# The 32-row forward substitutions of a hybrid decoder layer, issued on GpSimd (POOL) in place of VectorE (DVE)

## The chip, the cores and the metric

The kernel runs on one core of one Trainium2 chip. The metric is the device time of one execution in microseconds (us). Three executions of the kernel before took 1258.54 to 1261.52 us, median 1260.12 us. One execution was also profiled: it took 1260.07 us, of which 1258.4 us is the span from its first to its last recorded instruction. All times "at ... us" count from the start of that span.

Engines carry these names in the rows: PE is TensorE (matmuls), DVE is VectorE, ACT is ScalarE, POOL is GpSimd, SP is SyncE, which here only issues transfers (SPq is its queue).

## The reference: what is computed

One decoder layer on 256 tokens of width 2048, all in float32: a normalisation, one input product with `w_in`, four mixers side by side (gated delta rule, mLSTM, RG-LRU, RWKV-7), an output product with `w_out`, a SwiGLU feed-forward part, a last normalisation. Two mixers need a triangular solve per chunk. For the gated delta rule the reference says

```
lower = jnp.tril(jnp.einsum('nbhcd,nbhsd->nbhcs', kb, k) * decay, -1)
sol = lax.linalg.triangular_solve(lower + eye, rhs, left_side=True, lower=True, unit_diagonal=True)
```

and RWKV-7 is a scan over time, which the kernel turns into chunks with the same kind of solve.

## The kernel before

**Weights.** Every weight matrix is cut into 396 units of 128 x 1024 numbers. SP loads a unit into a `raw` buffer (4 of them), ACT copies it to `whi` (rounded to the matmul type), DVE computes `wlo = raw - whi`, and PE runs three matmuls for each product: whi with the activations' high part, whi with their low part, wlo with the high part (lines 169 to 171). There are 4 `whi` and 4 `wlo` buffers, so PE can be at most four units behind DVE. A unit of the input product is 24 matmuls, about 3 us of PE. These conversions carry line number 274, whatever engine they are on; a few carry 277. Tile names carry a number: `wlo_2268` is the low half of the unit whose high half is `whi_2267` and whose raw buffer is `raw_2265`.

**Mixers.** Their small work is written as Python generators (`rwkv_half`, `gdn_half`, `mlstm_half`, `rglru_half`, `gates_mm`, `joint_solve`) that are advanced a piece at a time between the units. From that program order, a scheduler with its own idea of how long each instruction takes makes one fixed order for each engine. Each engine then runs its list strictly in that order, and waits where an operand is not there.

**The solve.** `joint_solve` inverts many 32 x 32 unit triangular blocks at once, one block per partition: 64 blocks for RWKV, and later 32 for the delta rule. `blk` holds the blocks (loaded by lines 625 and 933), `inv` starts as the identity, and for each of 31 columns `solve_blocks` does two elementwise operations on 31 to 256 elements per partition: an outer product into `tmp` (line 499) and an addition into `inv` (line 500). Each reads what the one before wrote. Then line 503 writes the transpose of `inv` into `blk` with one copy on DVE, lines 512 and 513 store both to DRAM, and lines 660, 661 (RWKV) and 945, 946 (delta rule) load them back in another layout, for which lines 654, 940 and 941 have cleared the target on POOL.

**Neighbours in the DVE order.** `rglru_half` has the DVE lines 1140, 1150, 1151, 1154, 1155, 1158, 1161 and needs ACT for a square root (line 1152) between 1151 and 1154. `gates_mm` has the DVE lines 811, 814, 817, 818, and a scan at line 819, whose result PE transposes (line 413, tile `mx` from `sD`); ACT does a logarithm for it (line 816). The lines 763 and 774 are the convolution of the next column group and its activation, 1080 to 1088 belong to the mLSTM.

Of the kernel before, what the change touches and what calls it, by code (L numbers as in the profile page):

```python
# [10 lines left out]
ALU = mybir.AluOpType  # L11
# [478 lines left out]
def solve_blocks(em, q0, nq, steps, n=32):  # L490

    nc = em.nc
    blk, inv, tmp = em.blk[q0 : q0 + nq], em.inv[q0 : q0 + nq], em.tmp[q0 : q0 + nq]
    for j in range(n - 1):
        a, b = n - 1 - j, j + 1
        tv = tmp[:, 0 : a * b].rearrange("p (x y) -> p x y", x=a)
        col = blk[:, j, j + 1 : n].unsqueeze(2).to_broadcast([nq, a, b])
        row = inv[:, j, 0:b].unsqueeze(1).to_broadcast([nq, a, b])
        nc.vector.tensor_tensor(tv, col, row, op=ALU.mult)
        nc.vector.tensor_tensor(inv[:, j + 1 : n, 0:b], inv[:, j + 1 : n, 0:b], tv, op=ALU.add)  # L500
        if j % steps == steps - 1:
            yield
    nc.vector.tensor_copy(blk.rearrange("q s t -> q t s"), inv)


def joint_solve(em, key, q0, nq, steps, free=False):
    nc = em.nc
    while not all((key + "A", h) in em.mix for h in range(2)):
        yield
    yield from solve_blocks(em, q0, nq, steps)  # L510
    dt, dtt = (em.dp.tile([nq, 32, 32], F32, name=em.nm("dr"), tag=em.nm("dr")) for _ in range(2))
    nc.sync.dma_start(dt, em.inv[q0 : q0 + nq])
    nc.sync.dma_start(dtt, em.blk[q0 : q0 + nq])
    em.mix[key + "S"] = (dt, dtt)
    if free:
        em.free(*em.solver)
# [960 lines left out]
```

## Time and profile before

| | |
|---|---|
| median of 3 executions | 1260.12 us (1258.54 to 1261.52) |
| the profiled execution | 1260.07 us, span 1258.4 us |
| PE busy | 1237.0 us, 98% of the span |
| DVE busy | 788.2 us, 63% |
| ACT busy | 639.5 us, 51% |
| POOL busy | 32.7 us, 3% |
| substitutions on DVE | 124 instructions, 41.1 us, at 154 to 206 us (RWKV) and 356 to 411 us (delta rule) |
| granted TensorE clock, mean | 0.995 |

PE is busy almost all the time, so what counts is where PE has to wait. A busy share of another engine matters only where PE waits for that engine.

### The profile page before, as it was taken

The page shows a single profiled execution, that of the slowest core. Times are in us where ns is not written, and L with a number is a line of the kernel's source. Part 1 is how long each engine was busy: PE and PEld are TensorE (multiplying, and loading weights), DVE is VectorE, ACT ScalarE, POOL GpSimd, SP SyncE. Part 2 cuts the span into 40 slices and gives each one's busy share as a digit, 9 for nine tenths or more (in the row PEclk, how much of TensorE's full clock was granted, in tenths as well). Part 3 has the DMA queues.
Part 4 walks back from the last instruction along what each step waited for, and adds up shares of the span by engine and source line. Part 5 has one row for each costly group of instructions (what it writes and reads, how often), then busy time and mean ns, then how long its engine had stood idle before and what let it go on. Part 6 is the DMA issues. An engine that isn't in the chain of part 4 may idle for free.

```text
span 1258.4 us, 18347 instructions
## 1 busy us (share of the span) xinstructions
PE 1237.0 (98%) x7216; PEld 1066.3 (85%) x7216; DVE 788.2 (63%) x1096; ACT 639.5 (51%) x849; POOL 32.7 (3%) x65
## 2 busy tenths in 40 slices
PE   9999999999998999999999999999999999999997
PEld 8999999988998688888888888888888888878885
DVE  7896898668689767754454444444445465556554
ACT  7666774447644354644444444444444454455443
POOL 1000000000001010000000000000000000001000
PEclk9999999999999999999999999999999999999999
DMA  8664437363654635566666666666666666666663
GB/s 334 197 198 141 143 112 204 110 201 95 204 163 138 182 113 179 170 197 185 186 198 185 184 193 192 203 207 193 188 190 190 188 191 192 192 190 191 195 192 109
DMA packets 72198, 226.97 MB, mean 180 GB/s; under 512 B 15752, under 2 KB 16016, under 8 KB 72112
## 3 DMA queue, kind: packets, MB, share of 16 engines
q1 hardware_dynamic: 71504, 224.14, 58.3%
q0 software_dynamic: 464, 1.57, 0.5%
q8 instruction: 56, 0.92, 0.3%
q14 instruction: 30, 0.25, 0.1%
q10 hardware_dynamic: 144, 0.10, 0.0%
HBM read 222.49 MB, written 3.28 MB: 179 GB/s over the span
## 4 chain that ended last, share of the span: by engine, by line
PE 93%; DVE 4%; ACT 1%; issue 1%; DMA 0%; DVEq 0%; POOLq 0%; POOL 0%; SPq 0%; ACTq 0%
PE big L171 16%; PE big L170 16%; PE big L169 16%; PE mx L169 10%; PE mx L170 10%; PE mx L171 10%; PE mx L409 5%; PE big L277 2%; PE mxl L171 2%; PE mxl L170 2%; PE mxl L169 2%; DVE wlo L274 1%; PE mx L413 1%; DVE sA L763 0%; DMA sD<-in_xT 0%
## 5 line engine op out<-in xcount | busy, mean ns | idle before, releaser
L274 DVE TENSOR_TENSOR wlo<-raw,whi 128x1024 fp32r<-128x1024 f32 x396 | 485.4, 1227 | 356.5 <-ACT whi L274 355.5
L274 ACT ACTIVATE whi<-raw 128x1024 fp32r<-128x1024 f32 x396 | 417.8, 1057 | 431.0 <-PE big L171 296.5
L170 PE MATMUL big<-wlo,nhi 128*128 128x512 f32 (+1 forms) x464 | 161.4, 348 | 1.2 <-DVE wlo L274 1.2
L169 PE MATMUL big<-whi,nhi 128*128 128x512 f32 (+1 forms) x464 | 161.5, 348 | 0.0
L171 PE MATMUL big<-whi,nlo 128*128 128x512 f32 (+1 forms) x464 | 161.0, 347 | 0.0
L171 PE MATMUL big<-nhi,wlo 128*128 128x256 f32 x512 | 147.9, 289 | 0.0
L170 PE MATMUL big<-nlo,whi 128*128 128x256 f32 x512 | 147.9, 289 | 0.0
L169 PE MATMUL big<-nhi,whi 128*128 128x256 f32 x512 | 147.0, 287 | 0.0
L169 PE MATMUL mx<-whi,nhi 128*128 128x512 f32 x352 | 138.0, 392 | 0.0
L171 PE MATMUL mx<-whi,nlo 128*128 128x512 f32 x352 | 137.0, 389 | 0.0
L170 PE MATMUL mx<-wlo,nhi 128*128 128x512 f32 x352 | 137.0, 389 | 0.0
L170 PEld LDWEIGHTS big<-nlo,whi 128*128 128x128 f32 x512 | 97.7, 191 | 1.9 <-issue 0.7
L171 PEld LDWEIGHTS big<-nhi,wlo 128*128 128x128 f32 x512 | 97.7, 191 | 1.8 <-issue 0.3
L170 PEld LDWEIGHTS big<-wlo,nhi 128*128 128x128 f32 x464 | 88.5, 191 | 12.4 <-DVE wlo L274 1.6
L169 PEld LDWEIGHTS big<-nhi,whi 128*128 128x128 f32 x512 | 97.7, 191 | 1.2 <-issue 0.3
L169 PEld LDWEIGHTS big<-whi,nhi 128*128 128x128 f32 x464 | 88.4, 190 | 10.9
L171 PEld LDWEIGHTS big<-whi,nlo 128*128 128x128 f32 x464 | 88.5, 191 | 10.8
L170 PE MATMUL big<-wlo,sA 128*128 128x512 f32 x220 | 86.5, 393 | 3.7 <-DVE wlo L274 3.7
L169 PE MATMUL big<-whi,sA 128*128 128x512 f32 x220 | 86.7, 394 | 2.0 <-DVE sA L763 1.4
L169 PE MATMUL mx<-whi,sA 128*128 128x512 f32 x208 | 81.5, 392 | 0.7 <-ACT sA L1184 0.7
L170 PE MATMUL mx<-wlo,sA 128*128 128x512 f32 x208 | 81.0, 390 | 0.0
L171 PE MATMUL mx<-whi,sA 128*128 128x512 f32 x208 | 81.0, 389 | 0.0
(436 smaller groups left out, 1805.1 us busy)
## 6 DMA issues: line engine op xcount, KB each, us to landing
raw<-in_units SPq DMA_DIRECT2D x404, 512.0 KB, 3.7
sD<-in_x SPq DMA_DIRECT2D x8, 512.0 KB, 5.1
sD<-in_xT SPq DMA_DIRECT2D x4, 512.0 KB, 6.1
out_y<-sD SPq DMA_DIRECT2D x8, 256.0 KB, 3.0
sA<-in_final_norm POOLq DMA_DIRECT2D x4, 256.0 KB, 4.9
sD<-in_lora SPq DMA_DIRECT2D x1, 512.0 KB, 6.9
sD<-in_rglru POOLq DMA_DIRECT2D x1, 512.0 KB, 4.9
dr<-sD SPq DMA_DIRECT2D x2, 256.0 KB, 4.3
```

The source lines that it names most:

```text
L169: i = nc.tensor.matmul(out, ahi, bhi, start=start, stop=False, skip_group_check=True)
L170: nc.tensor.matmul(out, ahi, blo, start=False, stop=False, skip_group_check=True)
L171: self.last_mm = nc.tensor.matmul(out, alo, bhi, start=False, stop=stop, skip_group_check=True)
L274: i = fn(*a, **k)
L277: i = fn(*a, **k)
L409: return self.em.nc.tensor.matmul(*a, **k)
L413: return self.em.nc.tensor.transpose(*a, **k)
```

## The change

The two operations of each column of `solve_blocks` are issued on GpSimd. The copy of line 503 stays on VectorE.

```
@@ solve_blocks
         col = blk[:, j, j + 1 : n].unsqueeze(2).to_broadcast([nq, a, b])
         row = inv[:, j, 0:b].unsqueeze(1).to_broadcast([nq, a, b])
-        nc.vector.tensor_tensor(tv, col, row, op=ALU.mult)
-        nc.vector.tensor_tensor(inv[:, j + 1 : n, 0:b], inv[:, j + 1 : n, 0:b], tv, op=ALU.add)
+        nc.gpsimd.tensor_tensor(tv, col, row, op=ALU.mult)
+        nc.gpsimd.tensor_tensor(inv[:, j + 1 : n, 0:b], inv[:, j + 1 : n, 0:b], tv, op=ALU.add)
         if j % steps == steps - 1:
             yield
     nc.vector.tensor_copy(blk.rearrange("q s t -> q t s"), inv)
```

The scheduler makes new orders for all engines from this. On DVE, in the stretch of the RWKV solve, the order before had the substitutions strewn between other work (`sD_113` is `inv`, `sD_112` is `blk`, `sD_114` is `tmp`; `sA` and `sB` tiles are the RG-LRU's):

```order
L1140 TENSOR_TENSOR sA_271_2022<-sA_271_2022,sA_244_1801 128x512
L499 TENSOR_TENSOR sD_114_953<-sD_112_951,sD_113_952 64x220
L500 TENSOR_TENSOR sD_113_952<-sD_113_952,sD_114_953 64x22x10
L499 TENSOR_TENSOR sD_114_953<-sD_112_951,sD_113_952 64x231
L500 TENSOR_TENSOR sD_113_952<-sD_113_952,sD_114_953 64x21x11
L499 TENSOR_TENSOR sD_114_953<-sD_112_951,sD_113_952 64x240
L500 TENSOR_TENSOR sD_113_952<-sD_113_952,sD_114_953 64x20x12
L499 TENSOR_TENSOR sD_114_953<-sD_112_951,sD_113_952 64x247
L1150 SCALAR_TENSOR_TENSOR sB_275_2035<-sA_270_2021,sB_275_2035 128x512
```

In the order of the change the same place on DVE holds the copy of the finished inverse (`sD_278` is the gates' tile):

```order
L1140 TENSOR_TENSOR sA_271_2022<-sA_271_2022,sA_244_1801 128x512
L503 COPY sD_112_951<-sD_113_952 64x32x32
L1150 SCALAR_TENSOR_TENSOR sB_275_2035<-sA_270_2021,sB_275_2035 128x512
L814 TENSOR_SCALAR sD_278_2096<-sD_278_2096,gp 16x256
L1151 TENSOR_SCALAR sA_270_2021<-sB_275_2035 128x512
L811 TENSOR_SCALAR sD_278_2096<-sD_278_2096 16x256
L1156 MEMSET sA_274_2034 128x1
L1154 SCALAR_TENSOR_TENSOR sA_270_2021<-sB_275_2035,sA_270_2021 128x512
L1155 TENSOR_TENSOR sA_271_2022<-sA_271_2022,sA_270_2021 128x512
L1158 SCALAR_TENSOR_TENSOR sB_275_2035<-sA_274_2034,sA_271_2022 128x512
L817 TENSOR_TENSOR sD_278_2096<-sD_278_2096 16x256
L1161 TENSOR_TENSOR sB_275_2035<-sB_275_2035,sA_264_1972 128x512
```

The next three rows there are line 818, `wlo_2268` and the scan of line 819. Before, the copy stood 85 rows further down, behind eleven more units' `wlo`; it has moved up to the middle of where the substitutions were.

On DVE in the stretch of the delta rule's solve, before:

```order
L274 TENSOR_TENSOR wlo_4573<-raw_4570,whi_4572 128x1024
L500 TENSOR_TENSOR sD_113_952<-sD_113_952,sD_114_953 32x23x9
L499 TENSOR_TENSOR sD_114_953<-sD_112_951,sD_113_952 32x220
L500 TENSOR_TENSOR sD_113_952<-sD_113_952,sD_114_953 32x22x10
L499 TENSOR_TENSOR sD_114_953<-sD_112_951,sD_113_952 32x231
L500 TENSOR_TENSOR sD_113_952<-sD_113_952,sD_114_953 32x21x11
L274 TENSOR_TENSOR wlo_4620<-raw_4617,whi_4619 128x1024
```

and with the change:

```order
L274 TENSOR_TENSOR wlo_4573<-raw_4570,whi_4572 128x1024
L274 TENSOR_TENSOR wlo_4620<-raw_4617,whi_4619 128x1024
L503 COPY sD_112_951<-sD_113_952 32x32x32
L274 TENSOR_TENSOR wlo_4658<-raw_4655,whi_4657 128x1024
L1080 TENSOR_TENSOR dn_4523<-dn_4523,enm 128x2
```

Here too the copy has moved up, between two units' `wlo`, where before eleven of the 31 columns had been done.

On SP the stores and reloads of the RWKV inverse stood behind `raw_2902` before. With the change they stand between two weight loads ten units earlier (`sD_322` and `sD_326` are the reload targets of the two halves of the heads):

```order
L274 DMA raw_2404<-in_units 128x1024
L512 DMA dr_2510<-sD_113_952 64x1024
L513 DMA dr_2511<-sD_112_951 64x1024
L660 DMA sD_322_2514<-dr_2510 32x8x32 x2
L661 DMA sD_322_2514<-dr_2511 32x8x32 x4
L660 DMA sD_326_2552<-dr_2510 32x8x32
L661 DMA sD_326_2552<-dr_2511 32x8x32 x2
L660 DMA sD_326_2552<-dr_2510 32x8x32
L661 DMA sD_326_2552<-dr_2511 32x8x32
L822 DMA ncd<-sD_278_2096 4x256
L274 DMA raw_2443<-in_units 128x1024
```

On POOL the 62 substitutions of a solve stand in one run, each behind the one before; in the RWKV solve the two clears of line 654 stand among them. PE's order is the same up to the unit of `whi_2736`, ten units behind `whi_2267`; from there on the small matmuls that use the inverse stand earlier.

## Rows read from the trace of the kernel before

**Rows 1.** The page: busy us, share of the span and instructions by engine.

```profile
PE 1237.0 (98%) x7216; PEld 1066.3 (85%) x7216; DVE 788.2 (63%) x1096; ACT 639.5 (51%) x849; POOL 32.7 (3%) x65
```

**Rows 2.** Groups by line, DVE: count | busy us, mean ns of one.

```profile
L499 DVE TENSOR_TENSOR sD<-sD,sD 64x31 f32<-64x31 f32 (+31 forms) x62 | 20.5, 330 | 1.5
L503 DVE COPY sD<-sD 64x1024 f32<-64x1024 f32 (+1 forms) x2 | 2.3, 1126 | 0.0
```

**Rows 3.** Timeline of PE, 395 to 425 us: start, us, [idle before <-releaser].

```profile
403.41 0.52 PE L170 MATMUL big<-wlo,sA 128*128 128x512 f32 x1 [3.73 <-DVE wlo L274]
417.86 0.47 PE L169 MATMUL big<-whi,sA 128*128 128x512 f32 x1 [1.44 <-DVE sA L763]
```

**Rows 4.** Windows: length, busy us by engine, granted clock, DMA share, GB/s.

```profile
400.00:405.00 5.00, 1.59 (x4) 1.27 (x5) 4.73 (x10) 2.79 (x6) 1.34 (x2) 0.88 0.09 21
405.00:410.00 5.00, 5.00 (x21) 3.95 (x20) 4.68 (x11) 3.39 (x7) 0.00 (x0) 0.78 0.71 245
```

**Rows 5.** Timeline of SP, the loads of `blk`; the landing time of line 933.

```profile
146.14 0.31 SPq L625 DMA_DIRECT2D sD<-dr  x1
350.84 0.31 SPq L933 DMA_DIRECT2D sD<-dr  x1
DMA to landing us min/median/max: 3.4/3.4/3.4
```

**Rows 6.** POOL's own operations: timeline, and line 1348's durations.

```profile
3.65 0.45 POOL L307 TENSOR_TENSOR sA<-sA,ident 128x128 f32<-128x128 f32 x1
4.17 0.23 POOL L315 COPY gm<-strict 64x64 f32<-64x64 f32 x1
164.93 0.95 POOL L654 MEMSET sD<- 64x1024 f32 x1 [7.88 <-PE mx L409]
L1348 POOL TENSOR_TENSOR sD<-sD,sA x4: 1444/1740/2242, 1128.1 to 1134.8; 128x512 f32<-128x512 f32 x4
```

**Rows 7.** Timeline of POOL and DVE together, 1127 to 1138 us.

```profile
1130.87 5.65 POOL L1348 TENSOR_TENSOR sD<-sD,sA 128x512 f32<-128x512 f32 x3 [1.29 <-ACT sA L274]
...
1127.21 1.22 DVE L274 TENSOR_TENSOR wlo<-raw,whi 128x1024 fp32r<-128x1024 f32 x1
1130.14 0.69 DVE L1185 TENSOR_TENSOR sA<-sD,sA 128x512 fp32r<-128x512 f32 x1
1131.87 3.49 DVE L1185 TENSOR_TENSOR sA<-sD,sA 128x512 fp32r<-128x512 f32 x2
```

**Rows 8.** Windows ahead of the copy's new places; below, line 499 alone.

```profile
149.50:168.50 19.00, 19.00 (x156) 17.70 (x155) 18.33 (x40) 16.20 (x24) 1.90 (x2) 1.00 0.52 163
354.20:373.50 19.30, 19.30 (x162) 19.25 (x161) 17.58 (x39) 9.35 (x13) 0.00 (x0) 1.00 0.52 158
...
149.50:168.50 19.00, 2.50 (x9) 1.00 0.52 163
354.20:373.50 19.30, 3.32 (x11) 1.00 0.52 158
```

**Rows 9.** Timeline of DVE behind line 1140, and PE's wait point there.

```profile
171.96 0.69 DVE L1150 SCALAR_TENSOR_TENSOR sB<-sA,sB 128x512 f32<-128x512 f32 x1
179.42 0.67 DVE L819 TENSOR_TENSOR_SCAN sD<-sA,sD 16x256 f32<-16x256 f32 x1
...
180.72 0.48 PE L413 MATMUL mx<-ident,sD 16*128 16x16 f32 x5
```

**Rows 10.** Timeline of DVE and PE at `wlo_4658`.

```profile
376.53 1.22 DVE L274 TENSOR_TENSOR wlo<-raw,whi 128x1024 fp32r<-128x1024 f32 x1
...
381.60 0.28 PE L171 MATMUL big<-nhi,wlo 128*128 128x256 f32 x1
```

**Rows 11.** Timeline of SP, store and reload of the RWKV inverse.

```profile
207.75 0.45 SPq L513 DMA_DIRECT2D dr<-sD  x1
212.20 2.77 SPq L661 DMA_DIRECT2D sD<-dr  x6
216.55 0.40 SPq L274 DMA_DIRECT2D raw<-in_units  x1
```

More of the change, by code (lines that the diff above doesn't have):

```diff
@@ L498, in solve_blocks @@
         row = inv[:, j, 0:b].unsqueeze(1).to_broadcast([nq, a, b])
-        nc.vector.tensor_tensor(tv, col, row, op=ALU.mult)
-        nc.vector.tensor_tensor(inv[:, j + 1 : n, 0:b], inv[:, j + 1 : n, 0:b], tv, op=ALU.add)
+        nc.gpsimd.tensor_tensor(tv, col, row, op=ALU.mult)
+        nc.gpsimd.tensor_tensor(inv[:, j + 1 : n, 0:b], inv[:, j + 1 : n, 0:b], tv, op=ALU.add)
         if j % steps == steps - 1:
```

## The prediction, made before the changed kernel had run

> **What bounds the kernel now.** I read the busy times first: PE is busy for 1237 of 1258.4 us [rows 1], so a gain or a loss can only come from PE's waits. The waits of PE show where DVE is late today: PE stood 3.73 us for a `wlo` at 403.4 us and 1.44 us for a convolution at 417.9 us [rows 3]. Both lie in or just behind the stretch of the delta rule's solve, where DVE carries the substitutions beside the weights. After the first one the granted clock is 0.88 and 0.78 in two windows of 5 us, so for a while PE ran at 1.2 instead of 2.4 GHz: (0.12 + 0.22) x 5 = 1.7 us of PE's work lost [rows 4]. In the stretch of the RWKV solve PE waits for nobody: 19.00 of 19.00 us busy [rows 8]. So what DVE can give back is 3.7 + 1.4 + 1.7 = 6.8 us, though the substitutions take 62 x 0.33 us twice on it [rows 2].
>
> **What the change adds: a slow chain on POOL, with DVE waiting in order behind it.** The 62 operations of a solve depend on each other, so POOL does them one by one. Together they have 2 x the sum of (j+1)(31-j) over j = 0 to 30, that is 10,912 elements per partition. POOL's price is read from the two sizes of its own elementwise operations in this trace: 0.448 us (0.45 in the row) for 128 elements, 1.444 us for the fastest with 512 [rows 6]. That makes 1.0 us for 384 elements, 2.59 ns each, and 0.116 us that does not depend on the size. The instruction behind the first of them starts 0.07 us after its end [rows 6]. A solve is then 62 x 0.186 + 10,912 x 0.00259 = 11.5 + 28.3 = 39.8 us; the RWKV one has the two clears among its rows, 0.95 us each [rows 6]: 41.7 us. On DVE one solve took 62 x 0.33 = 20.5 us [rows 2], so POOL needs about twice DVE's time, and nothing of it runs side by side.
>
> When it can start: `blk` is sent for at 146.14 and at 350.84 us, and the second load lands after 3.4 us; with that for both, POOL starts at 149.5 and 354.2 us [rows 5].
>
> To this comes that the two engines hinder each other. While three POOL operations ran back to back, two DVE operations of a kind that alone takes 0.69 us took 3.49 us together, and the three took 5.65 us instead of 3 x 1.44 = 4.33 [rows 6, 7]. So POOL lost 1.3 us beside 2.6 us of DVE's own work (1.2 + 2 x 0.69): half of it. Ahead of the copy's new place DVE has, without the substitutions (18 and 22 of them; line 499 is half), 18.33 - 5.0 = 13.3 us and 17.58 - 6.6 = 10.9 us of work [rows 8]. I charge POOL with half, 6.6 and 5.4 us. DVE itself gets slower there too, but its `wlo` are some units ahead of PE's use (`wlo_4658` began 5.1 us before, [rows 10]), and it is on its way to a wait anyhow.
>
> POOL then ends at 149.5 + 41.7 + 6.6 = 197.8 us, and at 354.2 + 39.8 + 5.4 = 399.4 us.
>
> **Where that hits PE.** In the new DVE order the copy of line 503 stands directly behind line 1140, which DVE reaches about 169 us. DVE stops there for some 28 us. Behind it are, in this order, lines 1150, 814, 1151, the square root on ACT (which has the logarithm and `whi_2267` behind it, so ACT stands too), 1154, 1155, 1158, 817, 1161, 818, `wlo_2268`, and the scan of line 819. Each at its own step in that timeline (0.6 for 1150, 1154, 1155 and 1161, 0.3 to 0.4 for 814, 1151, 817 and 818, 0.7 for ACT with its handover, 1.14 for 1158, 1.13 for the `wlo`, 0.67 for the scan; first and last in [rows 9]) that is 7.4 us. PE's order is unchanged here: at 180.72 us it transposes the scan's result [rows 9], one instruction ahead of the end of its buffered units. So PE stands from 180.7 us until 197.8 + 1.1 (the copy, [rows 2]) + 7.4 = 206.3 us: **25.6 us**.
>
> The second time the copy stands between `wlo_4620` and `wlo_4658`. PE first used `wlo_4658` at 381.6 us, counted in units of 24 matmuls; DVE had made it at 376.5 us [rows 10]. Now it is ready at 399.4 + 1.1 + 1.1 = 401.6 us: **20.0 us**. The next `wlo` has lines 1080 to 1088 before it, some 3.7 us against a unit of 2.7 us on PE: 1.0 us more, an estimate.
>
> Both stalls are longer than the one at 403 us, after which PE lost 1.7 us to the low clock [rows 4]; I take that once for each, 3.4 us.
>
> SP also waits in order behind POOL now. Counted from the RWKV solve's end, the second store goes out at 1.2 us, the reload can start 4.45 us after it, and nine transfers take 4.35 us until a weight load goes out [rows 11]: 10.0 us. That load belongs to the fifth unit after PE's restart; with 3.7 us to land and 2.2 us for both halves it is ready at 16 us, and PE wants it about 22 us after the solve's end. That is hidden with some 6 us of cover; if every landing were 6 us later, SP would become the next wait. The reordered small matmuls of PE come later than that and have their data by then.
>
> **Sum.** 25.6 + 20.0 + 1.0 + 3.4 - 6.8 = +43.2 us. The profiled execution took 1260.07 us, 0.05 us from the median of the three, so the forecast is **1303 us**.
>
> **Bounds.** Without any hindrance it is 12 us less, 1291 us. If DVE's whole work in the two stretches delays POOL, it is 12 us more, 1315 us. POOL's rate: the 1.44 us operation began under a `wlo` that ran until 1128.4 us, 0.3 us after its start [rows 6, 7]; with 1.14 us in its place the rate is 1.8 ns and the fixed part 0.22 us, a solve 37.5 us, 2.3 us less each time. The slowest of the four took 2.24 us, 4.4 ns an element, which with the gaps makes 52 us a solve; it contains the hindrance, so 1291 + 2 x 12.3 = 1316 us. No POOL row reads with a broadcast or in rows of 1 to 31 elements 128 bytes apart, as these do. I take no surcharge, since the second addend's pattern is plain; for the range, half as much again on the 28.3 us is 14.1 us twice, 1332 us. Nothing suggests a gain from the pattern.
>
> **A rule that speaks to this.** The Trainium skill, "SBUF — State Buffer", section "Who interferes with whom", says that a DVE instruction with two SBUF inputs and a GpSimd instruction that reads SBUF shut each other out for their whole length. The doubled DVE operations at 1131.87 us agree with it. By that rule taken fully, the sum would be the 1315 us above instead of 1303.
>
> The Trainium skill, "GPSIMD Engine Reference", section "Elementwise — side-by-side cycle accounting", measures 4497 ns for 2048 elements of such an operation. By that, 2.2 ns an element, the sum would be some 9 us smaller, an estimate.
>
> **Rivals.**
> - *Faster: the chain fits.* If POOL finished the RWKV solve by 180.7 - 7.4 - 1.1 = 172.2 us, and the other by 381.6 - 2.2 = 379.4 us, no copy would hold PE, and DVE's relief would stay: 1260.1 - 6.8 = 1253 us. This needs a solve of at most 22.7 us with the clears, 0.34 us an operation. Against it: DVE itself needs 0.33, and POOL 0.45 for 128 elements where the mean here is 176. Chance 4%.
> - *Full exclusion or a dear pattern.* POOL and DVE take turns over the whole of both stretches, or narrow rows cost half as much again: 1313 to 1335 us. For it: the doubled DVE operations. Against it: POOL's own loss was half. 24%.
> - *A cheap POOL.* The low rate, no hindrance, and waits elsewhere that the stalls swallow (PE has 21 us idle in all): 1265 to 1288 us. 12%.
> - *No change.* The stalls would have to cancel the 6.8 us to within 2.5. 2%.
>
> My forecast, 1288 to 1313 us, has 58%. The range of 1285 to 1332 us holds that, most of the dear cases and a little of the cheap one, some 82%. What a measurement of this kernel can tell from no change is 0.2%, 2.5 us. From the cases above: faster than that 4%, the same 2%, slower 94%.
>
> **What would show it.** In the profile after, POOL should show 124 operations of 0.6 us on the mean and about 75 to 95 us of substitutions. DVE should be idle for 20 to 30 us ahead of each copy of line 503, released by POOL. PE should wait once in the input product for a transpose (line 413) and once for a `wlo`, some 20 to 26 us each, each with a lower granted clock behind it, and the waits at 403 and 418 us should be gone. If POOL's operations take under 0.35 us, or PE's two waits are under 5 us, the prediction is wrong; if the operations take 0.9 us, only its size.

## The result, and the profile of the changed kernel

The changed kernel took **1299.43 us** (median of 4, 1297.42 to 1300.6) against 1260.07 us (median of 4) for the kernel before on the same chip: 39.4 us more, a ratio of 1.031 (95% interval 1.0295 to 1.0325). Its profiled execution took 1297.42 us, with a span of 1295.7 us and a mean granted clock of 0.981.

Busy times on the page of the changed kernel (busy us, share of the span, instructions):

```profile
PE 1240.1 (96%) x7216; PEld 1069.5 (83%) x7216; DVE 755.5 (58%) x972; ACT 639.2 (49%) x849; POOL 109.6 (8%) x189
```

Beside [rows 1], DVE is 33 us lighter, POOL 77 us heavier, and PE has the same number of instructions; the span has grown by 37.3 us and PE's busy time by only 3.1, so PE stood for the rest. The waits of PE say where (total us, times, longest):

```profile
PE mx L413 <- DVE sD L819: 23.4, 1, 23.4
PE big L171 <- DVE wlo L274: 17.8, 1, 17.8
...
PE big L170 <- DVE wlo L274: 1.2, 1, 1.2
```

Two waits hold it all, and the waits of [rows 3] are gone. The third line, 1.2 us, is not the change's work: it stands at 338.56 us, and the kernel before has the same wait of 1.24 us at 311.59 us. Each of the two is read back over DVE to POOL. The timeline of DVE around both, and under it that of PE:

```profile
168.62 0.69 DVE L1140 TENSOR_TENSOR sA<-sA,sA 128x512 f32<-128x512 f32 x1 [1.04 <-ACT sA L1139]
195.66 1.03 DVE L503 COPY sD<-sD 64x1024 f32<-64x1024 f32 x1 [26.36 <-POOL sD L500]
196.54 0.66 DVE L1150 SCALAR_TENSOR_TENSOR sB<-sA,sB 128x512 f32<-128x512 f32 x1
...
203.41 0.67 DVE L819 TENSOR_TENSOR_SCAN sD<-sA,sD 16x256 f32<-16x256 f32 x1
...
422.26 1.43 DVE L503 COPY sD<-sD 32x1024 f32<-32x1024 f32 x1 [25.70 <-POOL sD L500]
423.73 1.22 DVE L274 TENSOR_TENSOR wlo<-raw,whi 128x1024 fp32r<-128x1024 f32 x1
```

```profile
204.14 0.60 PE L413 MATMUL mx<-ident,sD 16*128 16x16 f32 x4 [23.43 <-DVE sD L819]
...
425.00 0.58 PE L171 MATMUL big<-nhi,wlo 128*128 128x256 f32 x1 [17.79 <-DVE wlo L274]
```

DVE has nothing to do with the substitutions any more and yet stands 26.4 and 25.7 us at the copy, with line 1150 and everything behind it in the queue. From the copy's start to the end of the scan, the chain of [rows 9], 8.4 us pass, and PE follows at once. POOL itself, by groups (count | busy us, mean ns | idle before), and in its timeline at the ends and the middle of the two solves:

```profile
L500 POOL TENSOR_TENSOR sD<-sD,sD 64x31 f32<-64x31 f32 (+31 forms) x62 | 39.7, 641 | 4.9
L499 POOL TENSOR_TENSOR sD<-sD,sD 64x31 f32<-64x31 f32 (+31 forms) x62 | 38.2, 616 | 91.8 <-DMA sD<-dr 87.1
```

```profile
148.59 0.23 POOL L499 TENSOR_TENSOR sD<-sD,sD 64x31 f32<-64x31 f32 x1 [11.94 <-DMA sD<-dr]
...
165.53 1.49 POOL L500 TENSOR_TENSOR sD<-sD,sD 64x220 f32<-64x220 f32 x1
...
172.04 0.95 POOL L654 MEMSET sD<- 64x1024 f32 x1
...
185.18 0.61 POOL L500 TENSOR_TENSOR sD<-sD,sD 64x220 f32<-64x220 f32 x1
...
195.39 0.24 POOL L500 TENSOR_TENSOR sD<-sD,sD 64x31 f32<-64x31 f32 x1
...
379.79 0.23 POOL L499 TENSOR_TENSOR sD<-sD,sD 32x31 f32<-32x31 f32 x1 [75.18 <-DMA sD<-dr]
...
400.68 0.61 POOL L499 TENSOR_TENSOR sD<-sD,sD 32x252 f32<-32x252 f32 x1
...
404.26 0.73 POOL L500 TENSOR_TENSOR sD<-sD,sD 32x256 f32<-32x256 f32 x1
...
407.96 0.60 POOL L499 TENSOR_TENSOR sD<-sD,sD 32x247 f32<-32x247 f32 x1
...
421.99 0.24 POOL L500 TENSOR_TENSOR sD<-sD,sD 32x31 f32<-32x31 f32 x1
```

The same operation on 220 elements takes 1.49 us while DVE works and 0.61 us while DVE stands. The sizes of the 31 columns run up and down symmetrically, so one trace gives both prices: in the delta rule's solve the last 13 columns, with DVE idle, took 422.23 - 407.96 = 14.3 us, the middle five 7.3 us, the first 13, of the same sizes but beside DVE for most of the time, 20.9 us. POOL's own time is 2 x 14.3 + 7.3 = 35.8 us, and DVE cost it 6.6 us; in the RWKV solve the first 13 columns took 172.04 - 148.59 = 23.45 us, so 9.2 us.

Windows of 5 us behind the two waits (length, busy us by engine, granted clock, DMA share, GB/s):

```profile
204.00:209.00 5.00, 4.86 (x27) 4.83 (x28) 4.55 (x9) 2.19 (x4) 0.00 (x0) 0.59 0.76 240
425.00:430.00 5.00, 5.00 (x23) 5.00 (x24) 3.14 (x8) 4.11 (x10) 1.37 (x2) 0.50 0.58 193
```

PE comes back at the lower of its two levels, 1.2 GHz, for most of 5 us: 0.41 x 5 + 0.50 x 5 = 4.5 us of work lost.

### The profile page after: what moved, and what is told of

Same layout as the page of the kernel before. It is cut to its first block, busy times and chain, and to the rows that moved or that the text cites. A ratio compares the mean times of both kernels' runs of the same rounds, so it can differ in the third digit from the quotient of the medians.

```text
span 1295.7 us, 18350 instructions
## 1 busy us (share of the span) xinstructions
PE 1240.1 (96%) x7216; PEld 1069.5 (83%) x7216; DVE 755.5 (58%) x972; ACT 639.2 (49%) x849; POOL 109.6 (8%) x189
## 4 chain that ended last, share of the span: by engine, by line
PE 87%; POOL 6%; DVE 2%; issue 2%; ACT 1%; DMA 1%; SPq 0%; DVEq 0%; POOLq 0%; ACTq 0%
PE big L171 15%; PE big L170 15%; PE big L169 15%; PE mx L169 10%; PE mx L171 10%; PE mx L170 10%; PE mx L409 4%; POOL sD L500 3%; POOL sD L499 3%; PE big L277 2%; PE mxl L171 1%; PE mxl L170 1%; PE mxl L169 1%; DVE wlo L274 1%; DMA sD<-dr 0%
## 5 line engine op out<-in xcount | busy, mean ns | idle before, releaser
L171 PE MATMUL big<-nhi,wlo 128*128 128x256 f32 x512 | 150.0, 293 | 17.8 <-DVE wlo L274 17.8
L170 PE MATMUL big<-nlo,whi 128*128 128x256 f32 x512 | 149.5, 292 | 0.0
L171 PEld LDWEIGHTS big<-whi,nlo 128*128 128x128 f32 x464 | 87.7, 189 | 10.9
```

The source lines that it names most:

```text
L170: nc.tensor.matmul(out, ahi, blo, start=False, stop=False, skip_group_check=True)
L171: self.last_mm = nc.tensor.matmul(out, alo, bhi, start=False, stop=stop, skip_group_check=True)
```

## The experiments

Theories. **Order**: the time is waiting, because engines that run a fixed list stand at an instruction that needs POOL's result. **Contention**: the time is POOL and DVE hindering each other, wherever the copy stands. The two are not exclusive: what delays POOL's end also lengthens a wait for it. A third, **queue**, is that SP's stores become the next wait. The ratios are against the kernel before, run on the same chip.

**1. A chain on POOL that nobody waits for.** In the kernel before, behind each two substitutions on DVE (`spare` is a tile of its own, `ones` a constant tile that the rows call `rm`; code cut to the added operations):

```
+        w = min(a * b, 192)
+        nc.gpsimd.tensor_tensor(spare[:, 0:w], blk[:, 0, 0:w] if w <= 32 else ones[:, 0:w], spare[:, 0:w], op=ALU.mult)
+        nc.gpsimd.tensor_tensor(spare[:, 0:w], ones[:, 0:w], spare[:, 0:w], op=ALU.add)
```

> The kernel before, with its substitutions on DVE, and beside them on POOL a chain of 62 dependent operations per solve (up to 192 elements, on a tile of their own, added work that nobody waits for; the output is that of the kernel before). Order theory (the time of the change was lost because DVE's fixed order stands at the copy until POOL has finished): nothing here waits for POOL, so 1260 to 1266 us; the few us are the hindrance making DVE's weights later at 403 us, where PE already waited. Contention theory (the time was lost because POOL and DVE hinder each other at SBUF): POOL reads and writes beside DVE as in the change, DVE even has the substitutions as well, so most of the 39 us comes back: 1285 to 1300 us.

1291.18 us, ratio 1.0258 (1.0236 to 1.0279). Read by the expectation this is the contention theory, and my own reckoning was off by 25 us. The timelines of DVE and POOL at one place, and the group of line 503 (499 before), show more:

```profile
186.76 1.21 DVE L274 TENSOR_TENSOR wlo<-raw,whi 128x1024 fp32r<-128x1024 f32 x1
187.90 0.67 DVE L826 TENSOR_TENSOR_SCAN sD<-sA,sD 16x256 f32<-16x256 f32 x1
```

```profile
186.04 5.84 POOL L507 TENSOR_TENSOR spare<-rm,spare 64x192 f32<-64x192 f32 x1
191.96 0.65 POOL L506 TENSOR_TENSOR spare<-rm,spare 64x192 f32<-64x192 f32 x1
```

```profile
L503 DVE TENSOR_TENSOR sD<-sD,sD 64x31 f32<-64x31 f32 (+15 forms) x31 | 16.0, 516 | 0.4
```

One operation of POOL on 192 elements took 5.84 us while DVE ran its list without a gap, and the next one of the same size 0.65; DVE's substitutions took 516 ns on the mean where [rows 2] have 330. DVE still had its own 62 of them, so it was late for `wlo` and for the gates (PE's longest wait is 7.7 us, for the scan of line 819). (The group covers 148 to 222 us.) Nor is it quite a chain that nobody waits for. Its last multiplication reads `blk`, which DVE's copy overwrites next, and on POOL it stands ahead of `mrs`, a small operation of the mLSTM (line 1089 before) that ACT needs:

```profile
219.99 1.12 DVE L510 COPY sD<-sD 64x1024 f32<-64x1024 f32 x1 [1.81 <-POOL spare L506]
...
413.69 0.69 ACT L1099 ACTIVATE sA<-sA,mrs 128x128 f32<-128x128 f32 x2 [7.47 <-POOL mrs L1096]
```

The waits of PE that can come from this are small, 3.1 us for `whi` and 1.4 us for a reload. The run is no picture of the change, where DVE has no substitutions: it shows that the hindrance is real, not how much of the 39 us it is. Runs 9 and 10 ask that without these flaws.

**2 and 3. One solve alone on POOL.**

```
+    eng = nc.gpsimd if nq == 64 else nc.vector    # run 3: nq == 32
-        nc.gpsimd.tensor_tensor(tv, col, row, op=ALU.mult)
+        eng.tensor_tensor(tv, col, row, op=ALU.mult)
```

(and the addition alike)

> Only the RWKV solve (64 blocks) runs on POOL; the delta rule's stays on DVE. Order theory: one wait of PE of about 23.4 us for the transpose of line 413 with about 2.0 us of low clock behind it; the waits at 403 and 418 us of the kernel before stay: 1260.1 + 25.4 = 1285.5 us, range 1282 to 1290. Contention theory: no single wait, but many short waits for wlo between 150 and 196 us; by the share of POOL's hindrance there (9.2 of 15.8 us) some 23 us, 1283 us; so the two are told apart by the list of PE's waits, not by the total.

> Only the delta rule's solve (32 blocks) runs on POOL; the RWKV one stays on DVE. Order theory: one wait of PE for a wlo of 17.8 us with 1.2 us for the next and about 2.0 us of low clock, less the 6.8 us that the waits at 403 and 418 us cost before: 1260.1 + 21.0 - 6.8 = 1274.3 us, range 1271 to 1278. With the RWKV run the excess over 1260.1 should add up to the change's 39.4 us within 2 us. Contention theory: many short waits between 380 and 422 us, 16 us, 1276 us: again told apart by the list of waits.

1288.54 us, ratio 1.0228 (1.0211 to 1.0245), and 1271.11 us, 1.0089 (1.0074 to 1.0104). The longest wait of PE in run 2, and under it in run 3:

```profile
PE mx L413 <- DVE sD L820: 23.4, 1, 23.4
```

```profile
PE big L171 <- DVE wlo L274: 17.8, 1, 17.8
```

Each solve carries its own single wait, to the tenth of a us that of the change. The excesses over 1259.33 us are 29.2 and 11.8 us, together 41.0, beside the change's 39.4. The RWKV run is 3 us above its estimate. In its profiled execution POOL began 2.1 us later than in the change (at 150.73 against 148.59 us), behind a stretch from 110 to 115 us at a clock of 0.68 that the trace of the change does not have; where the rest lies was not settled. Both fit the order theory's ranges; the contention theory's totals were near, but it wanted many short waits.

**4. The copy later in DVE's order.** The unit's `wlo` is kept as `last_lo`, and

```
-    nc.vector.tensor_copy(blk.rearrange("q s t -> q t s"), inv)
+    with em.tc.issue_after(em.last_lo.ins):
+        nc.vector.tensor_copy(blk.rearrange("q s t -> q t s"), inv)
```

> As the change, but the copy of line 503 stands further back in DVE's order, behind the weight half that had been issued last when the solve was written, where POOL is expected to be done or nearly so; SP's stores stay at their early place, between two weight loads. Order theory with the queue as the next wait: DVE does not stand, but SP holds the next weight load until the copy has run and nine transfers are through; with four raw buffers ahead, PE waits for that load instead, 5 to 10 us per solve: 1265 to 1280 us, and PE's waits name a weight half that waited for its DMA. Order theory without the queue (SP's cover of 6 us is enough): 1253 to 1260 us. Contention theory: the two engines do the same work side by side as in the change, so 1290 to 1300 us.

1297.82 us, ratio 1.0302 (1.0285 to 1.0319): by the time alone this is the contention theory's figure, and the queue's is missed by 18 us. PE's longest waits, and the timelines of SP, DVE and ACT, one after the other:

```profile
PE mx L413 <- DVE sA L847: 21.4, 1, 21.4
PE big L169 <- ACT whi L274: 15.1, 1, 15.1
```

```profile
207.47 0.51 SPq L513 DMA_DIRECT2D dr<-sD  x1
```

```profile
217.28 1.22 DVE L274 TENSOR_TENSOR wlo<-raw,whi 128x1024 fp32r<-128x1024 f32 x1 [26.46 <-ACT whi L274]
```

```profile
430.38 0.69 ACT L1093 ACTIVATE sA<-sA,mrs 128x128 f32<-128x128 f32 x2 [23.15 <-POOL mrs L1090]
```

The traces say waiting again: the copy holds nobody now, and something else does. In the RWKV stretch SP stands at the store of `inv` until POOL ends at about 207 us; no weights come in, so ACT and DVE starve for 26 us. In the delta rule's stretch ACT stands 23 us at line 1093 (1092 before), whose operand `mrs` is a small operation of POOL itself, queued behind the solve; no theory had named that place. The queue theory names the right place in the RWKV stretch and has the size wrong. One reason is that POOL's solve took 55.7 us (151.7 to 207.4) in place of 47.0 (148.6 to 195.6), as DVE went on working beside it.

**5. The stores and reloads on POOL's queue as well.** As run 4, with `nc.sync` replaced by `nc.gpsimd` in lines 512, 513, 660, 661, 945 and 946.

> As the run with the late copy, but the stores of the inverse (lines 512, 513) and its reloads (660, 661, 945, 946) are issued on POOL's queue instead of SP's, so that no weight load stands behind them. If SP's queue was what took the place of DVE's wait (the weight loads behind the store stopped at 207 us there), the RWKV wait of 21.4 us goes and PE waits at most some 5 to 10 us for the reloaded inverse; the delta rule's wait of 15 us stays as long as ACT's line 1092 stands behind POOL's line 1089, which is queued behind the solve: 1270 to 1285 us. If POOL's speed beside DVE sets the time by itself, wherever the waiting instruction stands, it stays at 1292 to 1300 us.

1293.93 us, ratio 1.0273 (1.0249 to 1.0297), above the queue's range and in that of a time that POOL sets wherever the waiting instruction stands. PE's longest waits, and under them ACT's in its timeline:

```profile
PE big L169 <- ACT whi L274: 20.7, 1, 20.7
PE big L171 <- DVE wlo L274: 6.7, 2, 6.2
```

```profile
419.91 0.69 ACT L1093 ACTIVATE sA<-sA,mrs 128x128 f32<-128x128 f32 x2 [26.77 <-POOL mrs L1090]
```

The RWKV wait fell from 21.4 to 6.2 us. The 6.2 are not the reload, as expected (that costs 1.4), but DVE, which in this order stands at the copy again:

```profile
207.12 1.03 DVE L504 COPY sD<-sD 64x1024 f32<-64x1024 f32 x1 [13.82 <-POOL sD L500]
```

The wait behind POOL's `mrs` rose from 15.1 to 20.7 and took a part of the gain back: a store and three reloads now stand between the end of the solve (414.3 us) and `mrs` (419.2 us), which in run 4 followed after 1.1 us. Two queues, DVE's and ACT's, still stand behind POOL's solve here, and POOL's end sets the time.

**6 to 8. Every queue cleared.** The copy, the stores and the reloads of a solve go to POOL, so that only PE's small matmuls need POOL's result; run 6 for the RWKV solve alone, run 7 for the delta rule's alone, run 8 for both. In runs 7 and 8 also

```
-        nc.gpsimd.tensor_tensor(rs[:, g], ss[:, g], em.mhalf[:, 0:2], op=ALU.pow)
+        rsqrt_ln(em, rs[:, g], ss[:, g], 0.0)
```

> Only the RWKV solve on POOL, with its copy, stores and reloads on POOL too; the delta rule's solve stays on DVE, as in the kernel before. No queue of another engine waits for POOL, only PE's small matmuls that use the inverse. Order theory: PE's wait of 23.4 us goes; the solve ends at about 207 us beside a busy DVE, copy and transfers take some 12 us more, and PE's first use stands at some 213 us: a wait of 0 to 10 us, 1258 to 1272 us. Contention theory: as the run with the RWKV solve alone, 1285 to 1290 us.

> Only the delta rule's solve on POOL, with its copy, stores and reloads on POOL too, and line 1089 (the power -0.5 of the mLSTM's two sums, on POOL so far) done by a logarithm and an exponential on ACT, so that nothing that ACT or DVE needs is queued behind the solve; the RWKV solve stays on DVE, as in the kernel before. Order theory: no wait of 17.8 us, and DVE's relief stays: 1260.1 - 6.8 = 1253 us, range 1251 to 1259, where the upper end holds a wait of PE for the reloaded inverse. Contention theory: slowed weights on DVE make PE wait again, 1262 to 1272 us.

> Both solves on POOL with their copies, stores and reloads, and line 1089 on ACT as in the run before: every queue but POOL's is free of the solve. Order theory: the sum of the two runs before, 1251 to 1268 us, so 30 to 45 us of the change's 39 come back though POOL does all the work of the change and more. Contention theory: 1285 to 1300 us.

1279.44 us, ratio 1.0154 (1.0127 to 1.018); 1258.58 us, 0.9986 (0.9974 to 0.9998); 1277.63 us, 1.0144 (1.0121 to 1.0167). With both solves on POOL the change's 39 us shrink to 17, and run 7 is in its range, but only 1.7 us below the kernel before, less than the 2.5 us that the prediction took as the least that can be told from no change. Runs 6 and 8 end between the two theories. PE's waits in run 6, the windows behind them, and POOL's group there:

```profile
PE mx L409 <- DMA sD<-dr: 6.8, 1, 6.8
PE mx L413 <- DVE sD L821: 2.2, 1, 2.2
```

```profile
183.00:193.00 10.00, 9.93 (x62) 9.86 (x63) 6.64 (x12) 2.21 (x3) 9.45 (x8) 0.69 0.64 210
224.00:234.00 10.00, 8.49 (x108) 7.88 (x109) 1.95 (x3) 1.42 (x2) 1.69 (x3) 0.50 0.06 15
```

```profile
L501 POOL TENSOR_TENSOR sD<-sD,sD 64x31 f32<-64x31 f32 (+15 forms) x31 | 28.9, 933 | 2.4
```

With DVE never standing at the copy, the operations of line 501 (500 before) take 933 ns on the mean, where the same solve in run 2 took 650. The inverse reaches PE at 225.5 us, 6.8 us late; the waits of 2.2 and 6.8 us leave PE at a clock of 0.69 and 0.50 over 10 us each: 0.31 x 10 = 3.1 us, and half of the 8.5 busy us, 4.2 us. The wait for the inverse that I had put at 0 to 10 us is there; the 2.2 us for the scan and the 7.3 us of clock behind the two I had left out.

**9 and 10. The price of the hindrance where nobody waits.** No engine substitutes, so the inverse stays the identity and this part of the computation is missing; run 9 has in its place a chain on POOL with the sizes of the change, run 10 has not (code cut to the chain):

```
-        nc.vector.tensor_tensor(tv, col, row, op=ALU.mult)
-        nc.vector.tensor_tensor(inv[:, j + 1 : n, 0:b], inv[:, j + 1 : n, 0:b], tv, op=ALU.add)
+        nc.gpsimd.tensor_tensor(sv, blk[:, 0, 0:31] if j == 0 else ones[:, 0 : a * b], sv, op=ALU.mult)
+        nc.gpsimd.tensor_tensor(sv, ones[:, 0 : a * b], sv, op=ALU.add)
```

> The substitutions are left out altogether (the inverse stays the identity, so this part of the computation is missing); in their place POOL does 62 dependent operations of the same sizes as in the change on a tile that nobody reads, starting when the blocks have landed. The clears of lines 654, 940 and 941 go to DVE and line 1089 to ACT, so nothing waits for POOL. DVE has no substitutions, as in the change. Order theory: all that the change lost was waiting, so this takes 1251 to 1257 us (1260.1 less the 6.8 us of the waits at 403 and 418 us, plus up to 4 us of slower weights). Contention theory: POOL's reads beside DVE's weights cost by themselves, 1275 to 1300 us.

> The run before without POOL's chain: no substitutions on any engine (that part of the computation is missing). Both theories: 1251 to 1256 us. The difference to the run with the chain is what POOL's operations beside DVE cost when nobody waits for them: order theory 0 to 4 us, contention theory 20 to 45 us.

1261.68 us, ratio 1.0015 (1.0001 to 1.0029), and 1254.02 us, 0.9956 (0.9939 to 0.9972). So the chain beside DVE costs 7.7 us, twice what the order theory gave it at most, and far below the 20 to 45 us of the contention theory. In run 9's trace it shows at one place; PE's wait, and the window behind it:

```profile
PE mx L414 <- DVE sD L820: 4.6, 1, 4.6
```

```profile
185.00:190.00 5.00, 4.68 (x28) 4.64 (x29) 5.00 (x9) 1.15 (x2) 4.92 (x2) 0.66 0.69 203
```

The gates' chain, which PE needs at 180.7 us, comes 4.6 us late, and 0.34 x 5 = 1.7 us of clock follow. The profiled execution (1258.95 us) is the quickest of ten, 2.7 us below their median, so the trace need not show all of the 7.7 us. Run 10 is what DVE's relief is worth with nothing on POOL: 1259.97 - 1254.02 = 6.0 us.

**11. Clears in place of two-operand operations.** Run 1 with, for each two of POOL's added operations, four of

```
+            nc.gpsimd.memset(spare, 0.0)
```

> The kernel before with its substitutions on DVE, and beside each solve a run of 124 clears on POOL (192 elements each, no operand read; added work, the output is that of the kernel before) in place of the two-operand operations of the first added chain, which cost 31 us. If that chain cost because both engines read operands at the same time, POOL's clears cost nothing: 1259 to 1263 us. If any POOL instruction beside DVE costs, 1275 us or more.

1259.48 us, ratio 1.000 (0.999 to 1.001). POOL's group, count | busy us, mean ns:

```profile
L509 POOL MEMSET spare<- 64x192 f32 (+1 forms) x248 | 63.7, 257 | 14.2
```

63.7 us of POOL beside a full DVE cost nothing that can be measured, and DVE's substitutions of line 503 took 327 ns on the mean from 148 to 222 us, against 516 in run 1. The clears read nothing; the operations of run 1, which cost 32 us, read two operands. Operations on POOL that read one operand were not run.

**12. A later use.** Run 7 with two more pieces of other work ahead of PE's first use of the inverse:

```
-    for _ in range(4):
+    for _ in range(6):
         yield
     UU = em.S(c="B")
```

> As the run with only the delta rule's solve, copy, stores and reloads on POOL and line 1089 on ACT, but with two more pieces of other work between the reload and PE's first use of the inverse, some 13 units later in PE's order. Order theory: the two waits of 2.2 us for the reload and the 3.4 us of low clock behind them go, 1258.6 - 7.7 = 1251 us, range 1249 to 1256, unless the later use makes the end of the mixers late, which would show as a PE wait behind 450 us: 1257 to 1265.

**1249.74 us**, ratio 0.992 (0.9905 to 0.9935): the fastest of all. PE's busy time and its longest waits:

```profile
PE 1233.3 (99%) x7216; PEld 1064.1 (85%) x7216; DVE 769.5 (62%) x1033; ACT 651.4 (52%) x865; POOL 91.0 (7%) x140
```

```profile
PE mxl L274 <- DVE wu L274: 1.3, 1, 1.3
PE big L170 <- DVE wlo L274: 1.2, 1, 1.2
```

Nothing above 1.3 us is left: the two waits of 2.2 us of run 7 are gone, and so are those of [rows 3].

The kernel before took 1259.97 us on that chip, so the gain is 10.2 us, and DVE's relief alone does not explain it: run 10, where no engine substitutes at all, gains 6.0. Of the 11.0 us between the spans of the two profiled executions, 7.3 are idle time of PE, and 2.6 are low clock in windows of 5 us, of which run 12's trace has none; a part of the latter, 1.3 us at 310 us, is missing from the change's trace too. The remaining 1.1 us are open. A later use with the solve left on DVE was not run, so how much of the gain is POOL's doing is not shown.

## Why the prediction was right, step by step

| term | predicted us | measured us |
|---|---|---|
| POOL starts (RWKV) | at 149.5 | at 148.6 |
| POOL's own time, with the clears | 41.7 | 35.8 + 1.9 = 37.7 |
| hindrance, RWKV / delta rule | 6.6 / 5.4 | 9.2 / 6.6 |
| POOL ends (RWKV) | at 197.8 | at 195.6 |
| copy and chain to PE | 8.5 | 8.4 |
| PE's first wait | 25.6 | 23.4 |
| PE's second wait, and the next `wlo` | 20.0 + 1.0 | 17.8 + 0 |
| low clock behind both | 3.4 | 4.5 |
| DVE's relief | -6.8 | -6.0 (run 10) |
| sum | +43.2 | +39.7 (medians: +39.4) |

- **The mechanism** held: two waits, at the two places named, with the copy as the instruction that stands, and the waits at 403 and 418 us gone. Runs 2 and 3 show one wait for each solve, and run 8 that 22 us of the 39 go when nothing but PE's use of the inverse waits for POOL. The wait of 1.0 us for the next `wlo` did not come: PE has none between its restart at 425.0 us and 440 us. The low clock, taken over from the wait at 403 us, was sized too low, 3.4 against 4.5 us.
- **POOL's rate** was the term charged too high. It took 0.61 us for 256 elements and 0.23 for 31 on line 499, 0.73 and 0.24 on line 500: 1.7 and 2.2 ns an element, where [rows 6] gave 2.59. The fixed part is 0.17 us and the gap 0.08, where I had 0.116 and 0.07. The bound that took the `wlo` out of the 1.44 us operation, 1.8 ns with 0.22 us, was the nearer one. Reading with a broadcast shows no surcharge: line 499, which does it for both operands, is the cheaper.
- **The hindrance** was charged too low: two thirds of DVE's 13.3 us in the RWKV stretch and 0.6 of the 10.9, not half. The half itself left out the `wlo` that ran from 1135.29 us beside the last of the three POOL operations; with it they lost 1.3 us beside some 3.8 us of DVE's work, a third. The errors cancel in part, which is luck: POOL's own time was 8.0 us too long for both solves, the hindrance 3.8 us too short; with the measured rate and the half, the forecast would have been 1295 us, still in its range. The prediction rightly charged only DVE's work ahead of the copy; the expectation of run 4 forgot that DVE's stop bounds the term. Where DVE goes on, in run 6, the additions take 933 ns against the 650 of run 2. The full exclusion rival has less than its whole claim: not all of DVE's work delayed POOL.
- **SP's cover** was enough: no wait of PE names a late weight load. Run 4 shows the price once it is gone, 21.4 us instead of the 23.4 that the copy cost.
- **Contention** costs 7.7 us where nobody waits for POOL (runs 9 and 10). In the change it works through the waits instead: it made POOL end 9.2 and 6.6 us later, and PE's two waits of 23.4 and 17.8 us end with POOL's chain, so by this reckoning 15.8 of their 41.2 us are hindrance. Order decides that PE stands; how long it stands is POOL's own time and the hindrance together.

The Trainium skill, "SBUF — State Buffer", section "Who interferes with whom", says that a DVE instruction with two SBUF inputs contends with a GpSimd instruction that reads SBUF, and not with one that only writes it. Runs 1 and 11 agree, 32 us against none.

The Trainium skill, "GPSIMD Engine Reference", section "Elementwise — side-by-side cycle accounting", has 4497 ns for 2048 elements, which is 2.2 ns each by division, an estimate. Line 500 agrees with it, line 499 is below at 1.7.

## What to carry to other kernels

Moving a dependent chain to an idle engine moved its end here, and the first instruction that needed the end then stopped a whole in-order queue for 26 us: find that instruction on every engine, SP and the slow engine's own queue among them, before the move, since clearing one showed the next at nearly the same price (runs 4 and 5). The one version that paid (run 12, 0.8% faster) moves only the solve whose stretch had a late DVE, gives POOL everything up to the last reload and puts the use later in PE's order; which of these parts earns how much was not separated. Take the price of POOL's work beside a DVE that goes on working, not beside one that soon stands: 933 ns an addition in run 6 against 650 in run 2.

## What the runs showed of the hardware that I had not expected

- The hindrance goes to either side. An operation of POOL on 192 elements, 0.65 us elsewhere, was stretched to 5.84 us while DVE's `wlo` kept its 1.21 us (run 1); DVE's own short substitutions rose from 330 to 516 ns in the same run.
- Clears on POOL, 63.7 us of them, cost DVE nothing (run 11).
- A wait of 2.2 us was followed by a granted clock of 0.69 over 10 us, one of 6.8 us by 0.50 over 10 us, in which PE mostly ran 32 x 32 matmuls (run 6); the kernel before ran such matmuls from 213 to 228 us at 1.00. The second cost 4.2 us of work beside its 6.8 us of wait; behind the 23.4 us wait of the change it was 2.0 us.
